# A second buffer for the convolution rows, and two weight loads asked for one pair of heads earlier, in the attention stage of a decoder layer

## The chip, the cores and the metric

The kernel runs on one NeuronCore of a Trainium2 chip. That core has five engines with a queue of instructions each: PE (TensorE, the matmuls), DVE (VectorE), ACT (ScalarE), POOL (GpSimd) and SP (SyncE, which here only issues transfers). Transfers are issued from SP's and POOL's queues and run on the same 16 DMA engines. Every engine works through its queue in order, so an instruction that waits holds up all that stand behind it there. The metric is the device time of the program in microseconds (us), a median over runs.

## The reference

One layer over 1024 tokens of width 1024, in float32. First a mixer: one input projection feeds a sparse attention (8 heads of 64) and, beside it, a short gated convolution over 512 channels; both results are normalised and go through one output projection `w_out`. Then a cross-attention into 256 memory tokens, then a gated feed-forward network of width 2816.

```python
o_nsa  = nsa_attention(q, kc, vc, ks, vs, kw, vw, gates, ...)   # (S, 512)
u      = cc * cx
y      = sum(conv_w[k] * u_pad[:, 2 - k : 2 - k + S] for k in range(3))
o_conv = cb * y                                                 # (S, 512)
merged = concat([rmsnorm(o_nsa), rmsnorm(o_conv)], axis=-1)     # (S, 1024)
h      = merged @ w_out
x      = x + rmsnorm(h)            # then cross-attention, then SwiGLU
```

`w_out` has 1024 rows, so `merged @ w_out` is a sum of two halves: the 512 convolution rows, which are ready before the attention begins, and the 512 attention rows, which are not.

## The kernel before

All large products are made of three matmuls (`mm3`, lines 123 to 125): each operand is split into a high and a low part, and high by high, high by low and low by high are added up. The split takes one ACT copy (line 119) and one subtraction on DVE or POOL (line 120).

The program has these stages: input projections and convolution (up to about 311 us), attention (311 to 566 us), the output projection's attention half together with cross-attention (566 to about 800 us), the feed-forward network (the rest). The change is in the attention stage, and its effects reach the next.

The attention stage has 32 tasks: 8 tiles of 128 tokens, and 4 pairs of heads in each. `run_soft` makes a task's scores on PE (lines 650 and 651), adds the bias and takes the maximum on DVE (656 and 667), takes the exponential on ACT (658 and 688), and divides on POOL (695 for the window part `pwin`, 697 for the selected part `psel`). `pv_stage` transposes these on PE (line 720, into `t`), splits them on ACT and DVE (119 and 120, `pth` and `ptl`) and multiplies by the values (line 726, into `o`). The soft part runs two tasks ahead of the values. At the end of a tile POOL adds up the result `on` (line 738) and SP writes it to DRAM (line 741).

Between these, `fill` does the convolution half of `w_out`: 16 fills, two for each tile of 128 tokens. The first of a pair loads the tile's convolution rows `mhl` (a POOL transfer of 512 KB, line 773). Each fill is 12 matmuls into one bank `f`, an ACT copy to `stg` (line 782), and an SP transfer of `stg` to `pc_d` (line 783). There is one buffer for `mhl`, one for `f` and one for `stg`. `FILL = [5, 7, 10, 10, 12, 13, 13, 16, 16]` says how many fills are written down before each tile's tasks; the last three are written down after task 27.

The weights stand in six buffers named `big`. Four hold `wos[4]` to `wos[7]`, the convolution half, for the whole stage. `load_wo` (line 199) loads `wos[0]` to `wos[3]`, the attention half, 1024 KB each, from POOL's queue. The first two go to the free buffers; `wos[2]` and `wos[3]` take those of `wos[4]` and `wos[5]`, so these two transfers wait until the last fill has read them.

The order of instructions on each engine is not the order of the text. A scheduler places them by a simulated timeline and by the order of the text as priority; `issue_after` keeps a transfer behind a given instruction.

After the attention, `u_load` (lines 869 to 874) brings back, for one tile at a time, the attention result `on`, the fills' sums `pt` (written by `pc_d`) and the residual `x`, all from SP's queue, in the order tile 1, tile 0. `u_merge` splits `on` to `mh` and `ml`, and `u_proj` does 24 matmuls of three in `p` with `wos[0]` to `wos[3]`. These tiles lie in memory that the attention stage has used, so their loads wait for its last readers.

Of the kernel before, what the change touches and what calls it, by code (L numbers as in the profile page):

```python
# [10 lines left out]
F32R = mybir.dt.float32r  # L11
# [6 lines left out]
P = 128  # L18
# [48 lines left out]
def hymba_kernel(ctx: ExitStack, tc: tile.TileContext, a, out: bass.AP):  # L67
# [3 lines left out]
    def pool(st, name, bufs=1, side="left", space=None):  # L71
        kw = {"space": space} if space is not None else {"side": side}
        if space is not DRAM:
            kw["reuse_waits"] = "tile"
        return st.enter_context(tc.tile_pool(name=name, bufs=bufs, **kw))
# [46 lines left out]
    def mm3(ps, lh, ll, rh, rl, start, stop):  # L122
        T.matmul(ps, lh, rh, start=start, stop=False)  # L123
        T.matmul(ps, lh, rl, start=False, stop=False)  # L124
        T.matmul(ps, ll, rh, start=False, stop=stop)  # L125
# [66 lines left out]
    def big_tile():  # L192
        return big.tile([P, 4, 512], F32, name="big")
# [3 lines left out]
    def load_wo(k):  # L197
        wos[k] = big_tile().bitcast(F32R)
        Gp.dma_start(wos[k].rearrange("p a b -> p (a b)"), wo_d[k].rearrange("p x c -> p (x c)"))
# [369 lines left out]
    def group_stat(pl, pn, i, on):  # L569

        sq = pl.tile([P, 4, P], F32, name="sq", bufs=1)
        A.activation(sq, on, AF.Square)
        for c in range(4):
            T.matmul(pn, sq[:, c, :], ones[:, 0:1], start=c == 0, stop=c == 3)
        V.tensor_copy(gn[:, i:i + 1], rsqrt(small, pn, 512, 1, "gn"))


    ap2 = pool(at_stack, "ap2", bufs=2)
    with ExitStack() as st:
# [170 lines left out]
        def run_soft(n):  # L750
            if n >= len(tasks):
                return
            i, h0 = tasks[n]
            g = h0 // 4
            qi, pc, mb = cmps[i]
            if h0 % 4 == 0:
                nts[i, g] = near_stage(i, g, mb)
            yield from soft_stage(n, i, h0, qi, mb, nts[i, g])
            nx = ORD.index(i) + 1
            if h0 == CH and nx < NT:  # L760
                yield
                cmps[ORD[nx]] = cmp_stage(ORD[nx])
# [3 lines left out]
        def fill(m):  # L766

            if m >= 2 * NT:
                return
            i, n = divmod(m, 2)  # L770
            if n == 0:
                mhl = ap2.tile([P, 2, 4, P], F32R, name="mhl", bufs=1)
                Gp.dma_start(mhl.rearrange("p x c t -> p (x c) t"),
                             oc_d[:, :, :, i * P:(i + 1) * P].rearrange("p x c t -> p (x c) t"))
                oct_[i] = (mhl[:, 0], mhl[:, 1])
            mh, ml = oct_[i]
            ps = psf.tile([P, 512], F32, name="f")
            for k in range(4):
                w = wos[4 + k]
                mm3(ps, mh[:, k, :], ml[:, k, :], w[:, n, :], w[:, 2 + n, :], k == 0, k == 3)  # L780
            stg = ap2.tile([P, 512], F32, name="stg", bufs=1)
            A.activation(stg, ps, AF.Copy, scale=rc[:, i:i + 1])
            Y.dma_start(pc_d[i][:, n * 512:(n + 1) * 512], stg)
# [4 lines left out]
        for m in range(FILL[0]):  # L788
            fill(m)
        for n, (i, h0) in enumerate(tasks):  # L790
            ahead = run_soft(n + SKEW)
            pv = pv_stage(i, h0, cmps[i][1], *soft.pop(n))
            steps = next(pv)
            acc = OFF[i]
            for _ in pv:
                acc += RATE[i] / steps
                while acc >= 1:
                    acc -= 1
                    next(ahead, None)
            for _ in ahead:  # L800
                pass
            if n in (9, 21, 29, 30):
                with tc.issue_after(last["norm"].ins):
                    load_wo((9, 21, 29, 30).index(n))
            if h0 == H - 2:
                if i != ORD[-1]:
                    group_stat(ap2, psf.tile([P, 1], F32, name="f"), i, ons[i])
                for m in range(FILL[n // 4], FILL[n // 4 + 1]):
                    fill(m)
        for m in range(FILL[NT], 2 * NT):  # L810
            fill(m)
# [620 lines left out]
```

## Time and profile before

| what | value |
|---|---|
| median of 3 runs | 1412.88 us (1407.75 to 1414.35) |
| profiled execution, device time | 1411.98 us |
| its span in the trace | 1410.2 us |
| PE busy | 1344.6 us, 95% of the span |
| DVE busy | 939.1 us, 67% |
| ACT busy | 683.1 us, 48% |
| POOL busy | 468.1 us, 33% |
| HBM traffic | 143 GB/s over the span |

The span is the time in the trace from the first instruction to the last; some 1.8 us of the device time lie around it. A share of the whole span is a mean over stages that differ, so a stage has to be looked at by itself: which engine is full there, and what PE waits for at its ends. The page also gives the clock that PE was granted, as a share of full speed; its two levels are 2.4 and 1.2 GHz.

### The profile page before, as it was taken

Reading aid. Unit: us, or ns where it says so; the run is one execution under the profiler, and the core shown is the slowest. Engines: PE = TensorE matmul, PEld = TensorE weight load, DVE = VectorE, ACT = ScalarE, POOL = GpSimd, SP = SyncE. Lnnn points to the kernel's source line nnn. Section 1 sums busy time; section 2 is a strip of 40 time slices with the busy share of each in tenths; the row PEclk is TensorE's granted clock in tenths of the full one; section 3 lists DMA queues with packets and bytes.
Section 4 is the critical chain, followed back from the end, with each engine's and each line's share of the span. In section 5 each row is a group of like instructions: output and inputs, shape, how many; then the busy total and the mean of one; then the engine's idle time right before and its main releaser. Section 6 shows DMA issues by size and latency. Waiting matters only on the chain.

```text
span 1410.2 us, 19760 instructions
## 1 busy us (share of the span) xinstructions
PE 1344.6 (95%) x6748; PEld 1125.7 (80%) x6748; DVE 939.1 (67%) x2089; ACT 683.1 (48%) x1465; POOL 468.1 (33%) x454
## 2 busy tenths in 40 slices
PE   8999999999999999798789899999999999989997
PEld 6988888888889888687668688888888887867885
DVE  6544553346889996478886976545454444998787
ACT  5433334337878886356675533332333333444463
POOL 1232332227767664211220076555444531000000
PEclk9999999999999999899899999999999999999999
DMA  7488566495643302953236644432222226930213
GB/s 232 139 281 282 152 219 180 145 256 106 135 83 68 76 9 72 404 190 117 92 98 209 192 152 142 149 124 65 82 83 90 68 90 238 359 112 30 68 60 120
DMA packets 161061, 203.28 MB, mean 144 GB/s; under 512 B 8530, under 2 KB 115198, under 8 KB 156703
## 3 DMA queue, kind: packets, MB, share of 16 engines
q1 hardware_dynamic: 128416, 146.44, 32.3%
q0 software_dynamic: 31392, 53.48, 13.8%
q10 hardware_dynamic: 1152, 2.10, 0.4%
q8 instruction: 53, 0.87, 0.3%
q14 instruction: 48, 0.39, 0.1%
HBM read 138.54 MB, written 63.44 MB: 143 GB/s over the span
## 4 chain that ended last, share of the span: by engine, by line
PE 76%; DVE 13%; ACT 3%; issue 3%; DMA 2%; POOL 1%; SPq 0%; DVEq 0%; POOLq 0%; ACTq 0%
PE m L125 13%; PE m L124 13%; PE m L123 13%; PE mm L123 5%; PE mm L125 5%; PE mm L124 4%; PE o L726 3%; PE t L720 2%; DVE ptl L120 1%; PE s L650 1%; DVE psel L667 1%; PE s L651 1%; PE mm L228 1%; PE tr L485 1%; PE o L124 1%
## 5 line engine op out<-in xcount | busy, mean ns | idle before, releaser
L119 ACT ACTIVATE ah<-raw 128x512 fp32r<-128x512 f32 x132 | 83.0, 631 | 205.7 <-PE m L124 189.7
L125 PE MATMUL mm<-hh,wl 128*128 128x512 f32 x320 | 125.0, 392 | 1.3 <-POOL wl L120 1.3
L123 PE MATMUL mm<-hh,wh 128*128 128x512 f32 x320 | 126.2, 394 | 0.0
L124 PE MATMUL mm<-hl,wh 128*128 128x512 f32 x320 | 125.4, 392 | 0.0
L1169 POOL TENSOR_TENSOR sg<-sg,tmp 128x512 f32<-128x512 f32 x44 | 65.5, 1492 | 177.7 <-ACT sg L1163 67.4
L120 DVE TENSOR_TENSOR al<-raw,ah 128x512 fp32r<-128x512 f32 x120 | 107.6, 899 | 17.2 <-ACT ah L119 17.1
L124 PE MATMUL m<-bl,ah 128*128 128x512 f32 x264 | 102.7, 395 | 3.7 <-DVE bl L120 3.7
L125 PE MATMUL m<-bh,al 128*128 128x512 f32 x264 | 101.1, 394 | 3.0 <-DVE al L120 3.0
L120 POOL TENSOR_TENSOR wl<-wr,wh 128x1024 fp32r<-128x1024 f32 x22 | 54.0, 2454 | 133.2 <-ACT wh L119 133.1
L124 PE MATMUL m<-big,ah 128*128 128x512 f32 x232 | 91.6, 395 | 0.0
L120 DVE TENSOR_TENSOR ptl<-t,pth 128x512 fp32r<-128x512 f32 (+1 forms) x120 | 77.5, 656 | 15.9 <-ACT pth L119 15.8
L119 ACT ACTIVATE pth<-t 128x512 fp32r<-128x512 f32 (+1 forms) x120 | 66.9, 572 | 16.0 <-PE t L720 15.2
L123 PE MATMUL m<-bh,ah 128*128 128x512 f32 x264 | 72.0, 390 | 1.1 <-ACT bh L119 1.1
L125 PEld LDWEIGHTS mm<-hh,wl 128*128 128x128 f32 x320 | 60.5, 189 | 14.9 <-POOL wl L120 2.2
L123 PEld LDWEIGHTS mm<-hh,wh 128*128 128x128 f32 x320 | 60.6, 189 | 12.5
L124 PEld LDWEIGHTS mm<-hl,wh 128*128 128x128 f32 x320 | 60.7, 190 | 12.4
L124 PEld LDWEIGHTS m<-bl,ah 128*128 128x128 f32 x264 | 50.1, 190 | 15.8 <-DVE bl L120 5.3
L125 PEld LDWEIGHTS m<-bh,al 128*128 128x128 f32 x264 | 49.8, 190 | 14.8 <-DVE al L120 4.7
L1168 DVE TENSOR_TENSOR tmp<-m,t 128x512 f32<-128x512 f32 x40 | 27.6, 691 | 50.8 <-PE m L125 22.9
L119 ACT ACTIVATE ah<-q 128x512 fp32r<-128x512 f32 (+2 forms) x55 | 30.0, 545 | 60.5 <-PE m L124 58.6
L123 PEld LDWEIGHTS m<-bh,ah 128*128 128x128 f32 x264 | 49.5, 188 | 12.0 <-ACT bh L119 1.6
L1161 DVE TENSOR_TENSOR sg<-m,t 128x512 f32<-128x512 f32 x40 | 27.6, 691 | 44.4 <-PE m L125 39.6
(497 smaller groups left out, 4130.3 us busy)
## 6 DMA issues: line engine op xcount, KB each, us to landing
raw<-in_ffn_wg_dram SPq DMA_DIRECT2D x52, 256.0 KB, 3.0
raw<-in_ffn_wu_dram SPq DMA_DIRECT2D x52, 256.0 KB, 3.0
hid_d<-sg SPq DMA_DIRECT2D x22, 512.0 KB, 3.1
q<-in_ffn_wd_dram SPq DMA_DIRECT2D x44, 256.0 KB, 5.6
q<-hid_d SPq DMA_DIRECT2D x44, 256.0 KB, 5.4
wr<-in_w_in_dram SPq DMA_DIRECT2D x20, 512.0 KB, 4.5
x<-in_x_dram SPq DMA_DIRECT2D x16, 512.0 KB, 4.5
wo_d<-phl POOLq DMA_DIRECT2D x8, 1024.0 KB, 6.6
```

Of the source, the lines that this page charges most:

```text
L119: A.activation(hi, src, AF.Copy)
L120: (lo_eng or V).tensor_tensor(lo, src, f(hi), OP.subtract)
L123: T.matmul(ps, lh, rh, start=start, stop=False)
L124: T.matmul(ps, lh, rl, start=False, stop=False)
L125: T.matmul(ps, ll, rh, start=False, stop=stop)
L228: T.matmul(ps, rbB[:, h, :], oh, start=True, stop=True)
L485: T.matmul(ph, w1[:, c, :], xv[:, :, n0:n0 + 65, s0], start=c == 0, stop=c == 15)
L720: T.transpose(ps[:, m, j, :], pt[:, j, off * P:(off + 1) * P], ident)
L726: T.matmul(pof, vst[:, kt, b, g, :], t[:, m].rearrange("p h q -> p (h q)"), start=u + x + m == 0, stop=x == 1 and u + m == len(units) - 1)
L1161: V.tensor_tensor(dst, src0, src1, OP.add)
L1168: V.tensor_tensor(tmp, src0, src1, OP.add)
L1169: Gp.tensor_tensor(dst, dst, tmp, OP.mult)
```

## The change

`mhl` gets two buffers, so that the convolution rows of the next tile can be loaded while the fills of the last one still read theirs. And `load_wo` is asked for `wos[2]` after task 28 and `wos[3]` after task 29, where it was after 29 and 30.

```diff
             if n == 0:
-                mhl = ap2.tile([P, 2, 4, P], F32R, name="mhl", bufs=1)
+                mhl = ap2.tile([P, 2, 4, P], F32R, name="mhl", bufs=2)
                 Gp.dma_start(mhl.rearrange("p x c t -> p (x c) t"),
...
-            if n in (9, 21, 29, 30):
+            if n in (9, 21, 28, 29):
                 with tc.issue_after(last["norm"].ins):
-                    load_wo((9, 21, 29, 30).index(n))
+                    load_wo((9, 21, 28, 29).index(n))
```

Neither adds or takes away an instruction. Both move instructions, since the scheduler goes by when a buffer is free. Three places follow, each with the rows of one engine's queue before and then after.

PE, first tile of the attention. `s` are scores against the keys `ks` or `kw`, `t` transposes, `o` products with the values, `f` a fill (`f_2622` is the third, the first that needs the second tile's rows `mhl_2620`). Before:

```order
L650 MATMUL s_2738<-kw_1728,qi_2442 128x128
L651 MATMUL s_2738<-kw_1728,qi_2442 128x128
L708 MATMUL t_2780<-ident_64,pcx_2479 128x128 x2
L726 MATMUL o_2672<-ptl_2715,vst_103 128x256 x2
L650 MATMUL s_2743<-ks_1727,qi_2442 128x128
L651 MATMUL s_2743<-ks_1727,qi_2442 128x128
L650 MATMUL s_2748<-ks_1727,qi_2442 128x128
L651 MATMUL s_2748<-ks_1727,qi_2442 128x128
L123 MATMUL f_2622<-big_2348,mhl_2620 128x512
L124 MATMUL f_2622<-big_2348,mhl_2620 128x512
```

After:

```order
L650 MATMUL s_2687<-kw_1728,qi_2442 128x128
L651 MATMUL s_2687<-kw_1728,qi_2442 128x128
L720 MATMUL t_2709<-ident_64,pwin_2484 128x128 x2
L720 MATMUL t_2709<-ident_64,psel_2483 128x128 x2
L708 MATMUL t_2724<-ident_64,pcx_2479 128x128 x2
L123 MATMUL f_2622<-big_2348,mhl_2620 128x512
L124 MATMUL f_2622<-big_2348,mhl_2620 128x512
```

The third fill now stands 19 rows further up, ahead of five pairs of score matmuls and the first products with the values. On POOL, the load of `mhl_2620` has moved from behind the divisions of the first two tasks to directly behind the load of the first tile's rows.

PE, the end of the attention: the beginning of the last fill, `f_5765`. `psel_5816` belongs to the last but one task, `pwin_5939` and `psel_5938` to the last. Before:

```order
L720 MATMUL t_6122<-ident_64,pwin_5939 128x128 x3
L726 MATMUL o_6034<-ptl_6110,vst_103 128x256
L720 MATMUL t_6122<-ident_64,pwin_5939 128x128
L720 MATMUL t_6136<-ident_64,pwin_5939 128x128 x2
L720 MATMUL t_6136<-ident_64,psel_5938 128x128 x2
L123 MATMUL f_5765<-big_2348,mhl_5747 128x512
L124 MATMUL f_5765<-big_2348,mhl_5747 128x512
```

After:

```order
L720 MATMUL t_6056<-ident_64,pwin_5817 128x128
L726 MATMUL o_5781<-ptl_6024,vst_103 128x256
L720 MATMUL t_6056<-ident_64,pwin_5817 128x128
L720 MATMUL t_6056<-ident_64,psel_5816 128x128 x2
L720 MATMUL t_6069<-ident_64,psel_5816 128x128 x4
L123 MATMUL f_5765<-big_2348,mhl_5747 128x512
L124 MATMUL f_5765<-big_2348,mhl_5747 128x512
```

The last fill has moved up by one task. From its end to the first matmul of `p` there were 14 transposes and 23 products; now there are 34 and 46.

POOL, the same stretch; `wo_d2_84` and `wo_d3_85` are the sources of `wos[2]` and `wos[3]`, and `on_5905` is the last tile's result. Before:

```order
L697 TENSOR_SCALAR psel_5938<-psel_5938,sm_5941 128x1024 x2
L773 DMA mhl_5747<-oc_d_77 128x8x128
L738 TENSOR_TENSOR on_5905<-otmp_6027 64x256 x2
L199 DMA big_6032<-wo_d2_84 128x2048
L199 DMA big_6115<-wo_d3_85 128x2048
L738 TENSOR_TENSOR on_5905<-otmp_6197 64x256 x2
L816 DMA big_6203<-wq_d0_78 128x2048
```

After:

```order
L697 TENSOR_SCALAR psel_5940<-psel_5940,sm_5943 128x1024 x2
L738 TENSOR_TENSOR on_5905<-otmp_6029 64x256
L199 DMA big_5906<-wo_d2_84 128x2048
L738 TENSOR_TENSOR on_5905<-otmp_6029 64x256
L199 DMA big_6034<-wo_d3_85 128x2048
L738 TENSOR_TENSOR on_5905<-otmp_6197 64x256 x2
L816 DMA big_6203<-wq_d0_78 128x2048
```

The load of the last tile's convolution rows is gone from here (it stands 47 rows further up, among the divisions of the fifth tile). The two weight loads still stand behind the last division, one now between the two halves of an `on`. The order on SP from the last `pc_d` to the loads of `on`, `pt` and `x` for the next stage is the same in both.

## Rows read from the trace of the kernel before

**Rows 1.** The page: span, and busy time by engine.

```profile
span 1410.2 us, 19760 instructions
PE 1344.6 (95%) x6748; PEld 1125.7 (80%) x6748; DVE 939.1 (67%) x2089; ACT 683.1 (48%) x1465; POOL 468.1 (33%) x454
```

**Rows 2.** Windows: stretch, length, engines' busy time, granted clock, DMA share, GB/s.

```profile
311.00:350.00 39.00, 36.06 (x234) 32.35 (x233) 26.67 (x149) 27.67 (x88) 23.65 (x39) 0.96 0.57 108
...
450.00:500.00 50.00, 47.92 (x355) 45.04 (x354) 48.98 (x186) 41.37 (x96) 33.30 (x40) 1.00 0.31 69
500.00:550.00 50.00, 48.26 (x345) 43.90 (x344) 44.51 (x154) 42.99 (x95) 31.14 (x35) 1.00 0.05 17
...
650.00:700.00 50.00, 38.52 (x231) 33.16 (x230) 43.80 (x110) 35.51 (x107) 9.34 (x11) 0.90 0.27 96
700.00:750.00 50.00, 43.02 (x224) 35.83 (x224) 37.68 (x74) 32.63 (x81) 10.94 (x10) 0.90 0.42 135
```

**Rows 3.** Chain that ended last, pieces: start, length, what.

```profile
324.96 5.17 DMA mhl<-oc_d
...
564.57 6.08 DMA on<-on_d
```

**Rows 4.** Timeline of PE, 328 to 331 us: start, length, idle before in brackets.

```profile
328.50 0.28 PE L651 MATMUL s<-ks,qi 128*128 128x128 f32 x1
330.18 0.50 PE L123 MATMUL f<-big,mhl 128*128 128x512 f32 x1 [1.40 <-DMA mhl<-oc_d]
```

**Rows 5.** Timeline of POOL: two loads of `mhl`, and of `wos[2]`, `wos[3]`.

```profile
324.96 0.95 POOL L773 DMA_DIRECT2D mhl<-oc_d  x1
...
548.43 0.96 POOL L773 DMA_DIRECT2D mhl<-oc_d  x1
...
559.23 1.25 POOL L199 DMA_DIRECT2D big<-wo_d  x2 [7.69 <-PE f L125]
```

**Rows 6.** Timeline of PE, 560 to 578 us.

```profile
560.63 0.40 PE L125 MATMUL f<-big,mhl 128*128 128x512 f32 x1
...
565.29 0.28 PE L726 MATMUL o<-ptl,vst 128*128 128x256 f32 x1
571.35 0.80 PE L123 MATMUL p<-big,mh 128*128 128x512 f32 x1 [5.78 <-ACT mh L119]
...
573.22 0.63 PE L123 MATMUL p<-big,mh 128*128 128x512 f32 x1
573.64 0.63 PE L124 MATMUL p<-big,mh 128*128 128x512 f32 x1
...
577.02 0.40 PE L123 MATMUL p<-big,mh 128*128 128x512 f32 x1
577.25 0.39 PE L124 MATMUL p<-big,mh 128*128 128x512 f32 x1
```

**Rows 7.** Timeline of SP's queue, 545 to 565 us.

```profile
545.71 16.44 SPq L783 DMA_DIRECT2D pc_d<-stg  x3
562.25 0.46 SPq L870 DMA_DIRECT2D on<-on_d  x1
564.19 0.32 SPq L872 DMA_DIRECT2D pt<-pc_d  x1
```

**Rows 8.** DMA, 558 to 575 us: GB/s in 40 slices, the two queues.

```profile
GB/s 386 29 0 0 0 58 251 0 308 386 386 463 366 424 405 328 308 386 443 443 284 357 405 453 439 381 400 429 419 424 443 395 424 342 178 439 390 386 439 390
...
q0 software_dynamic: 386, 2.90, 50.0%
q1 hardware_dynamic: 1048, 2.70, 42.1%
```

**Rows 9.** Transfers of `on`, then of `pc_d`: issue to landing.

```profile
DMA to landing us min/median/max: 2.0/8.7/10.1
...
DMA to landing us min/median/max: 2.0/5.0/6.2
```

**Rows 10.** Waits, 311 to 575 us: total, times, longest.

```profile
ACT stg L782 <- DMA pc_d<-stg: 2.8, 2, 1.9
```

## The prediction, made before the result was known

> **What bounds the kernel now.** I read the page first: PE is busy for 95% of the span [rows 1], so time can come back only where PE stands still or runs at the lower clock, and only if nothing else is full there. The windows by stage come next [rows 2]. The reader is to see two things in them. From 450 to 500 us DVE is busy for 48.98 of 50 us, more than PE with 47.92: both are full, and a transfer that comes sooner gives nothing there. At the stage's two ends DVE has room (26.67 of 39 us from 311 to 350), and DMA is nearly unused before the last end (0.05 of the engines, 17 GB/s, from 500 to 550).
>
> Then the chain that ended last. In the attention stage two transfers stand on it: one of `mhl` at 324.96 us and one of `on` at 564.57 us [rows 3]. They are the two places that this change can reach, and PE's timeline shows what they cost. At 330.18 us the third fill begins after 1.40 us without work, waiting for `mhl` [rows 4]. At the end the last product with the values begins at 565.29 us and takes 0.28 us; the first matmul of `p` begins at 571.35 us, after 5.78 us of idle time [rows 6]. The matmuls behind it run at the lower clock level, 1.2 GHz: 573.22 to 573.64 us is 0.42 us from one to the next, 577.02 to 577.25 us is 0.23 us [rows 6].
>
> Last, why `on` was late. SP issues the fills' last `pc_d` just before 562.25 us, then the first `on`, then `pt` at 564.19 us; the second `on` goes out at 564.57 us [rows 3, 7]. POOL issues both weight loads at 559.23 us, having waited 7.69 us for the last fill [rows 5]. From about 561 us on the DMA engines move some 390 GB/s without a pause [rows 8]. The two weight loads are 2.1 MB; what SP had asked for up to the second `on` (`pc_d` 0.26, `on` 0.26, `pt` 0.52, `on` 0.26) is 1.3 MB. So `on` travels in a queue, not alone: 6.08 us, where the fastest `on` took 2.0 us [rows 3, 9].
>
> **The change, part by part.** No instruction is added or removed, so busy time stays; the sum is of waits. It is made against the profiled execution, 1412.0 us (a span of 1410.2 us and 1.8 us around it), which lies 0.9 us under the median of the runs, 1412.9 us.
>
> First fills. With two buffers the second tile's rows are asked for at about 305 us instead of 324.96 us, so the wait of 1.40 us goes [rows 4, 5]: -1.4 us. What is late next is `stg`, which still has one buffer: a fill's copy waits for the transfer of the fill before, 5.0 us in the median [rows 9], and the fills now follow each other sooner. Before, this was two waits of 2.8 us together, on ACT [rows 10], whose exponentials and splits queue behind the copy. I count the third to the fifth fill and the last two as likely to wait 0.5 to 1 us more each, of which PE feels a third, since transposes already in its queue go on: +1.2 us, between 0 (ACT's waits are covered) and +4 us (all of them reach PE).
>
> The middle. Fills keep their place to within some 30 matmuls. Where PE and DVE are both full [rows 2] I take 0. The bounds are -2 us (all that PE stands still from 450 to 500 us) and +2.8 us (one fill, 12 matmuls of 0.23 us, set ahead of scores for which DVE waits).
>
> Last fills. The last load of `mhl` went out at 548.43 us, behind the last divisions [rows 5]; now it stands 47 rows earlier, and the last fill can run one task earlier. Behind the last fill there are now 80 matmuls of the value part where there were 37. Those 37 took 4.7 us (560.87 to 565.57 us [rows 6]), so the 80 take some 10 us. `wos[4]` and `wos[5]` are therefore free about 11 us before the end of the attention, not 6, and the two weight loads go out then, when DMA is nearly idle, and need 5.4 us (2.1 MB at 390 GB/s), which ends before `pt` and the second `on` are asked for. Asking at tasks 28 and 29 alone would only let POOL wait longer; it is the earlier fill that makes the request worth something. The loads stand behind the last division, so nothing that PE needs is queued behind their wait.
>
> The boundary. `pt` still waits for the last transposes, 1.4 us before the attention's end, and `on` follows it. With the weights out of the way, 0.79 MB at 390 GB/s take 2.0 us, and with the 2.0 us of a transfer that is alone [rows 9] `on` lands at 564.19 + 4.0 = 568.2 us where it landed at 570.65 us: -2.4 us. Bounds: 0 (`on` is held by something that the chain doesn't name) and -4.1 us (2.0 us instead of 6.08).
>
> The Trainium skill ("DMA: Bandwidth & Descriptors", section "Queues, rings and completion order") says that each DMA engine takes turns between the queues that have work for it, packet by packet. By that rule SP's 1.3 MB would have had half the rate: 6.7 us from 561.8 us and 2 us of latency give 570.5 us, and the row has 570.65 us; both queues moved nearly the same (2.90 and 2.70 MB [rows 8]). The trace agrees, and by the same rule the landing without the weights is the 568.2 us above.
>
> The clock. Thirteen matmuls of `p` ran at the lower level, 0.42 instead of 0.23 us each: 2.6 us [rows 6]. With 3.4 us of idle time instead of 5.8 I take a third of it back, -0.9 us, between 0 and -2.6.
>
> Sum: -1.4 + 1.2 + 0 - 2.4 - 0.9 = -3.5 us, or 1409.4 us against the median. The next stage then starts 3.5 us earlier, with its order changed in some two dozen small places; I take 0 for it, and its bounds are in the rivals.
>
> **The rivals.** *The wait is taken up elsewhere.* `on` still stands behind `pt` and the first `on`; if the rest of the DMA work (5.60 MB in 17 us [rows 8]) fills the gap that the weights leave, and `stg` takes the start's gain, the result is -0.5 us: 1412.4 us. For it speaks that the engines are full to the end of that stretch; against it, that `wq` and all that follows on POOL is asked for only after the last `on` is added up, later than the loads on the chain.
>
> *Slower: fills ahead of scores.* The scheduler now puts the third to fifth fill before scores that DVE waits for. Each is 2.8 us on PE; DVE starts its later tasks up to 8.3 us later, and from 450 to 500 us it has hardly any room to catch up [rows 2]. If all of it stays, less the 1.4 us and the 3.3 us of the boundary, +3.6 us are left (8.3 - 1.4 - 3.3). PE would then wait for scores and fall to the lower clock as it did after 565 us; one and a half times that loss, 3.9 us, makes +7.5 us: 1420.4 us. The change is slower as soon as more than 4.7 us of the delay survive until POOL is past the last divisions, at 548 us [rows 5]. Against it: PE loses nothing while it does fills, and in 311 to 350 us DVE stood still for 12 of 39 us anyway.
>
> *Faster: the next stage.* From 650 to 750 us the granted clock is 0.90 [rows 2]: a fifth of 100 us at half speed, 10 us lost, and PE is busy for only 81.5 of the 100 us. There short waits decide on the clock, and another order and start can spare some of them. Two thirds of that loss on top of the forecast: 1402.7 us. Nothing in the trace says that the new order is better rather than worse, so this is a spread to both sides.
>
> *The change does nothing there*, because `mhl` still comes late, can be left out: for the last tile its transfer stands 47 rows of POOL further up than before.
>
> **How the numbers follow.** Chances: the forecast 0.43, taken up elsewhere 0.23, slower 0.13, faster by the next stage 0.21. What a measurement of this kernel can tell from no change is about 0.5%, 7 us, as far apart as its three runs lie. Faster than that (under 1405.8 us) is most of the last case, and a little of the forecast: 0.20. Slower (over 1420 us): 0.10, some of the slow case ending under it. Within: 0.70. The range reaches down past the faster case and up to where half of the slower one is in: 1401 to 1418 us. The forecast's own range is 1404 to 1415 us: its bounds add up to -10 and +7 us, and not all of them will fall to one side.
>
> **What would show it.** Right: no wait of `f` for `mhl` at 330 us; the weight loads on POOL some 11 us before the last product with the values; DMA busy between 550 and 560 us; the second `on` landing in about 4 us, and PE's wait for `mh` 3 to 3.5 us. Wrong: `on` still taking 6 us or more; more than 6 us of ACT waiting on `pc_d`; DVE standing still for longer than before between 450 and 500 us; or a difference that lies behind 600 us, which none of my terms is about.

## The result: the changed kernel is slower

The changed kernel takes 1427.1 us (1423.9 to 1430.2 in six runs), the kernel before 1412.3 us (1407.8 to 1414.4 in six): a ratio of 1.011, interval 1.0095 to 1.0125. The forecast was 1409.4 us, its range 1401 to 1418. The page of the profiled execution after answers to [rows 1]; the engines are as busy in sum, but for PE's 6 us more.

```profile
span 1425.6 us, 19754 instructions
PE 1350.5 (95%) x6748; PEld 1128.9 (79%) x6748; DVE 937.9 (66%) x2089; ACT 683.5 (48%) x1465; POOL 468.4 (33%) x454
```

**Where the 15 us are.** PE does the same matmuls in both kernels, so the traces can be laid on each other by work done: each matmul has the price of its form at full speed (0.23 us for 512 columns, 0.12 for 256, 0.09 for a transpose), the prices are added up in each kernel's own order, and the lag is how much later a kernel has done the same amount. Other prices move it by up to 0.5 us. One execution differs from the next by more: `e2` (below), whose instructions stand as in the kernel before, lies up to 0.7 us off it, and `e4`, the same up to the last fills, up to 1.1 us. The profiles differ by up to 3 us at 311 us already, ahead of all that is edited; that is taken off. Times at the top are those of the kernel before.

```
lag of PE, us, at            338   356   398   490   540   584   680   830
changed kernel              -1.5   3.8   3.5   8.2   7.7   3.5  10.7  14.8
```

So there are five pieces: a gain of 1.5 us at the first fills; 5.3 us lost by 356 us; 4.2 us lost between 398 and 540; 4.2 us gained at the boundary; and 11.3 us lost in the next stage, behind everything that the edit names.

**The gain at the start came.** The third fill begins without a wait; in [rows 4] it had 1.40 us.

```profile
326.43 0.48 PE L123 MATMUL f<-big,mhl 128*128 128x512 f32 x1
```

**The first loss.** The chain of waits of the changed kernel shows POOL's issue of one load and the transfer of another near 335 us; in [rows 3] its transfer was one of `mhl`, at 324.96 us (start, length, what):

```profile
335.24 0.95 POOL mhl L773
...
336.19 8.20 DMA qi<-q_d
...
344.53 0.27 PE s L592
```

`qi` are the queries of the next tile (line 588), here the third. They have two buffers, so the load waits until the last scores of the first tile are made. POOL's timeline, first two rows of the kernel before (the load of the second tile's rows is in [rows 5]), then the changed one:

```profile
329.08 1.14 POOL L588 DMA_DIRECT2D qi<-q_d  x1 [3.17 <-PE s L651]
330.58 1.04 POOL L606 TENSOR_TENSOR pc<-pc,csm 128x512 f32<-128x512 f32 x1 [0.36 <-DVE sm L692]
```

```profile
310.69 0.88 POOL L773 DMA_DIRECT2D mhl<-oc_d  x1 [5.37 <-PE mm L125]
...
325.20 0.95 POOL L773 DMA_DIRECT2D mhl<-oc_d  x1
329.74 1.04 POOL L606 TENSOR_TENSOR pc<-pc,csm 128x512 f32<-128x512 f32 x1 [3.59 <-DVE csm L605]
...
334.00 1.28 POOL L120 TENSOR_TENSOR pcx<-pc,pcx 128x512 fp32r<-128x512 f32 x1
335.24 0.95 POOL L773 DMA_DIRECT2D mhl<-oc_d  x1
336.19 1.14 POOL L588 DMA_DIRECT2D qi<-q_d  x1
```

The queries are asked for 7.1 us later. PE's timeline of the changed kernel shows when the scores that they wait for are made, and what the lateness costs:

```profile
334.50 0.28 PE L651 MATMUL s<-ks,qi 128*128 128x128 f32 x1
...
342.61 0.39 PE L726 MATMUL o<-pth,vst 128*128 128x256 f32 x1 [0.61 <-ACT pth L119]
...
344.53 0.27 PE L592 MATMUL s<-kcst,qi 128*128 128x64 f32 x1 [1.30 <-DMA qi<-q_d]
...
346.22 0.40 PE L592 MATMUL s<-kcst,qi 128*128 128x64 f32 x1
346.44 0.40 PE L593 MATMUL s<-kcst,qi 128*128 128x64 f32 x1
```

The last scores of the first tile begin at 334.50 us, behind the third and fourth fill; before, at 328.50 [rows 4]: 6.0 us later. On POOL the load has moved back as well. It stood ahead of the product for `pc` (line 606) and waited 3.17 us for the scores; now it stands behind that, behind a task's divisions and behind `pcx`, on which POOL is busy to 335.28 us, half a microsecond longer than the last scores take (to 334.78). So POOL's own work ends last, by little, and the late scores alone would hold the load nearly as long; no run holds the one and frees the other. The last 0.95 us are the load of the fourth tile's rows, which now stands just ahead of the queries on POOL. From 345.5 us on the matmuls go at half the pace (0.21 us apart, then 0.11 again from 352): PE fell to the lower clock level behind these waits.

**The second loss.** DVE's waits from 380 to 500 us (total, times, longest), of the kernel before and of the changed one:

```profile
DVE psel L667 <- PE s L651: 1.5, 4, 0.5
DVE pwin L656 <- PE s L651: 1.1, 1, 1.1
```

```profile
DVE pc L599 <- PE s L593: 3.7, 3, 2.4
DVE psel L667 <- PE s L651: 3.6, 4, 2.1
...
DVE pwin L656 <- PE s L651: 1.5, 2, 1.1
```

DVE waits 8.8 us for scores where it waited 2.6. In PE's order fills 9, 10, 11 and 12 stand ahead of 2, 4, 6 and 6 pairs of score matmuls against `ks` and `kw` that they stood behind, and fills 9 and 10 ahead of 8 and 2.5 pairs against the compressed keys (lines 592 and 593) too. DVE's longest wait is for those, behind fill 10:

```profile
398.87 0.23 DVE L599 CUSTOM_DVE_ANT_0 pc<-s,ct 128x64 f32<-128x64 f32 x1 [2.42 <-PE s L593]
```

The windows that answer to [rows 2] have DVE 3.0 us short from 311 to 350 us, 1.9 us from 450 to 500, and busier from 500 to 550; PE's clock in the next stage is down to 0.79:

```profile
311.00:350.00 39.00, 35.54 (x210) 31.72 (x210) 23.67 (x134) 23.57 (x74) 21.04 (x36) 0.90 0.70 117
450.00:500.00 50.00, 46.92 (x340) 42.83 (x339) 47.05 (x173) 39.87 (x94) 32.19 (x38) 1.00 0.47 90
500.00:550.00 50.00, 48.66 (x350) 44.38 (x349) 47.13 (x175) 44.35 (x97) 31.69 (x37) 1.00 0.03 12
650.00:700.00 50.00, 38.22 (x222) 32.35 (x222) 39.37 (x97) 34.42 (x101) 8.52 (x11) 0.90 0.23 85
700.00:750.00 50.00, 36.78 (x189) 30.40 (x188) 41.09 (x87) 33.25 (x89) 11.82 (x10) 0.79 0.31 95
```

**The boundary came as forecast, 7 us late.** POOL's weight loads, SP's transfers, and PE (answering to [rows 5 to 7]):

```profile
561.22 0.61 POOL L199 DMA_DIRECT2D big<-wo_d  x1
...
562.59 0.57 POOL L199 DMA_DIRECT2D big<-wo_d  x1
```

```profile
571.23 0.32 SPq L872 DMA_DIRECT2D pt<-pc_d  x1
571.60 0.42 SPq L870 DMA_DIRECT2D on<-on_d  x1
```

```profile
572.57 0.28 PE L726 MATMUL o<-ptl,vst 128*128 128x256 f32 x1
576.04 0.49 PE L123 MATMUL p<-big,mh 128*128 128x512 f32 x1 [3.20 <-ACT mh L119]
...
577.90 0.63 PE L123 MATMUL p<-big,mh 128*128 128x512 f32 x1
578.33 0.63 PE L124 MATMUL p<-big,mh 128*128 128x512 f32 x1
...
581.64 0.40 PE L123 MATMUL p<-big,mh 128*128 128x512 f32 x1
581.88 0.39 PE L124 MATMUL p<-big,mh 128*128 128x512 f32 x1
```

The last product is 7.28 us later than in [rows 6], the first matmul of `p` only 4.69. PE waits 3.20 us instead of 5.78, and some eight matmuls run at the lower level (0.43 us apart) instead of thirteen: 2.6 of the 4.2 us are the wait, the rest is the clock.

### The profile page after: what moved, and what is told of

Its sections match the earlier page's. It is cut to its first block, busy times and chain, and to the rows that moved or that the text cites. A ratio compares the mean times of both kernels' runs of the same rounds, so it can differ in the third digit from the quotient of the medians.

```text
span 1425.6 us, 19754 instructions
## 1 busy us (share of the span) xinstructions
PE 1350.5 (95%) x6748; PEld 1128.9 (79%) x6748; DVE 937.9 (66%) x2089; ACT 683.5 (48%) x1465; POOL 468.4 (33%) x454
## 4 chain that ended last, share of the span: by engine, by line
PE 78%; DVE 12%; issue 3%; ACT 3%; DMA 2%; POOL 1%; SPq 0%; DVEq 0%; POOLq 0%; ACTq 0%
PE m L125 13%; PE m L124 13%; PE m L123 13%; PE mm L123 6%; PE mm L125 6%; PE mm L124 6%; PE o L726 2%; PE t L720 2%; DMA x<-in_x_dram 1%; DVE ptl L120 1%; PE s L650 1%; PE s L651 1%; DVE psel L667 1%; PE mm L228 1%; PE tr L485 1%
```

## The experiments

Each kernel was timed beside the kernel before. The interval of its ratio to it stands with each, and the lags of their profiles (to be read as above) in one table at the end of this section. "Order held" means that the instructions of a stage are chained, engine by engine, in a given order, by dependences that carry no semaphore; in such kernels every instruction has line 76, that of the helper that records it.

```diff
+        for x, y in zip(at, at[1:]):
+            tc.add_manual_dep(logs[k][y], logs[k][x].name,
+                              mybir.DependencyInfo(mybir.DependencyClass.NoSync, mybir.DependencyReason.DATA),
+                              reason="order")
```

Here `logs[k]` lists the instructions of one engine as they are written down, and `at` is the order to hold.

**The two edits apart.** First theory: the second buffer alone costs it. `e1` has only the buffers, `e2` only the requests.

```diff
-            if n in (9, 21, 28, 29):
+            if n in (9, 21, 29, 30):
```

> Two buffers for the convolution rows, the weight blocks asked for as before (tasks 29 and 30). Theory: the whole loss comes from the second buffer, which lets the third to fifth fill stand ahead of scores; only one row of POOL's queue differs from the changed kernel, so attention ends at 572.5 us (573 within 1 us) and the time is the changed kernel's, 1427 us (1423 to 1431). Rival, the earlier requests cost it (weight blocks in the way of on and x): 1412 us or less.

> One buffer, the weight blocks asked for after tasks 28 and 29. Theory: the requests still stand behind the last division and wait for the last fill, no row of any queue moves against the kernel before, so 1412 us (1408 to 1416) and weight loads at 559 us. Rival, the earlier requests cost the 15 us: 1420 us or more.

Measured: 1426.4 us (1.0098 to 1.0132) and 1410.4 us (0.9993 to 1.0012). The buffers are the whole effect. The earlier requests move no instruction of any engine: they wait for the last fill in either case.

**The last fills alone.** `e4` has the early load only where the forecast needed it.

```diff
-                mhl = ap2.tile([P, 2, 4, P], F32R, name="mhl", bufs=2)
+                mhl = ap2.tile([P, 2, 4, P], F32R, name="mhl" if i < 7 else "mhe", bufs=1)
```

> One buffer for the rows of the first seven tiles, one of its own for the last tile's; requests after tasks 28 and 29. Only the last fills move. Theory, that the loss of the attention comes from the first fills: the attention ends at 565.5 us within 0.5, the boundary gives its 3 us (on lands in about 4 us, PE waits 3 us for mh). The next stage tells two things apart: if its 11 us in the changed kernel come from being late, 1409 us; if they come from its changed order (80 rows of PE and of DVE moved) it loses here too, 1413 to 1420 us.

Measured: 1409.8 us (0.9983 to 1.0007). The attention is level, and the boundary gives 3 us that last. (The lag of -5.8 us at 584 passes: the lower clock level, which the kernel before has from 570 to 577 us, comes here only at 592 us.) The next stage, in an order that is neither the old nor the changed kernel's, takes as long as before: 268.8 us for the work of the windows below. That speaks for lateness or for the changed kernel's own order, and the next four kernels take the next stage apart.

**The next stage: order or lateness?** `p1` is the changed kernel with the next stage's order held as before; `p4` the inverse.

> The changed kernel, with the instructions behind the attention stage (those written after line 818) held on every engine in the order that they have in the kernel before; the attention stage is the changed one. In the changed kernel PE is 3.7 us behind at 580 us and 15 us behind at 830 us. If the 11 us come from the changed order of the next stage: attention ends at 572 to 573 us as in the changed kernel, then PE stays about 4 us behind, 1415 to 1418 us. Rival, that they come from being late (transfers of x and on that meet others, the clock): 1424 us or more.

> The inverse: the kernel before, with the instructions behind the attention stage held in the order of the changed kernel. If the order costs the 11 us: attention ends at 565.5 us, time 1419 to 1423 us. Rival, that lateness costs it: 1409 to 1413 us.

Measured: 1415.7 us (1.0018 to 1.0041) and 1422.0 us (1.0061 to 1.0091). Both fall where the order was to put them: of the 15 us, 11 are the order of the next stage, wherever the attention ends. Windows from the first matmul of `p` to the same piece of work in the feed-forward network, of the kernel before, of `p4` and of the changed kernel:

```profile
571.40:840.00 268.60, 239.34 (x1197) 198.30 (x1198) 205.25 (x408) 151.37 (x374) 56.32 (x49) 0.93 0.53 178
```

```profile
569.20:848.80 279.60, 245.81 (x1197) 203.60 (x1198) 203.29 (x408) 151.77 (x374) 57.45 (x49) 0.90 0.51 171
576.00:855.00 279.00, 242.62 (x1197) 200.62 (x1198) 205.26 (x408) 151.87 (x374) 60.61 (x55) 0.91 0.51 172
```

The same 1197 matmuls take 11.0 us more in `p4`: 4.5 us of standing still (33.8 against 29.3 us) and 6.5 us of longer matmuls (245.8 against 239.3 us busy, mean clock 0.90 against 0.93). In the changed kernel the shares are the other way round, 7.1 and 3.3 us. The sum is steady: this work takes 267 to 269 us in all eleven kernels whose next stage has the order of before, and 279 to 280 in the three with the changed order (the changed kernel, `e1`, `p4`). The waits of PE that grew most in the windows of the kernel before and of `p4` are those of the transposes for `pr`, the normalised probabilities of the cross-attention:

```profile
PE s L972 <- DVE pr L958: 3.6, 3, 3.0
```

```profile
PE s L76 <- DVE pr L76: 6.8, 4, 4.0
```

Which engine's order carries it? `r4` changes PE's alone, `r6` DVE's and ACT's alone.

> The kernel before, with PE's order behind the attention stage as in the changed kernel, and the other engines as before. If PE's own order carries the 11 us of the next stage: 1418 us or more. If it is the order on DVE and ACT: 1410 to 1414 us.

> The inverse: DVE and ACT behind the attention stage in the order of the changed kernel, PE, POOL and SP as before. If DVE's and ACT's order carries the 11 us: 1418 us or more. If it is PE's: 1410 to 1414 us. If both kernels of this pair are slow, it is the two orders not fitting each other, and neither engine alone.

Measured: 1423.1 us (1.0077 to 1.0107) and 1425.2 us (1.0086 to 1.0119). Both are as slow as the whole changed order or slower, so the two kernels do not say which engine carries it: an order that is changed on one side alone no longer fits the other side's, and that may cost as much by itself. The whole changed order, in which all engines come from one schedule, costs the same, and what makes it slow stays open. The lag grows in several steps of 1 to 5 us between 600 and 810 us, not at one place.

**The attention: the order or the buffer?** `p5` has both edits, with PE, DVE and ACT held in the order of before through the program; `q4` the same, but with the last fills where the early load lets them stand (the order of `e4`), and the next stage held.

> Two buffers and the earlier requests, but PE, DVE and ACT keep the order of the kernel before through the whole program (POOL and SP are left to the scheduler, and differ in the one load of the last tile's rows). If the second buffer costs only by the order that it brings: 1409 to 1412 us, attention's end at 564 to 566 us, no wait longer than before. Rival, that the second buffer itself costs (its place in memory, its transfers beside the queries'): 1417 us or more.

> Two buffers and the earlier requests, with PE, DVE and ACT held in the order of the kernel that moved only the last fills, and the next stage in the order of the kernel before. If order is all that the change cost, both gains are left: the third fill's wait (1.4 us) and the boundary (3 us): 1405 to 1408 us. Rival, that the first gain is taken up by the wait for divisions or by the copies of stg: 1408 to 1410 us.

Measured: 1411.5 us (0.9994 to 1.0014) and 1407.8 us (0.9974 to 0.9997). The buffer costs nothing where it moves nothing. `q4` keeps the boundary's gain; the first fill's 1.7 us are there at 338 us and gone at 346 us. What takes them is neither of the two that its rival named, but mostly the clock: PE waits once, 0.47 us up to 336.69 us, and the granted clock is at the lower level from 338.2 to 341.6 us, which costs half of these 3.4 us.

```profile
338.00:342.00 4.00, 4.00 (x20) 3.82 (x19) 3.53 (x25) 2.75 (x9) 1.79 (x4) 0.57 0.16 30
```

**The early stall.** `e3` keeps the second tile's load behind the second task's division; `q1` lets it go early but holds the third fill's first matmul behind the first tile's last scores (next stage held).

```diff
-                Gp.dma_start(mhl.rearrange("p x c t -> p (x c) t"),
...
+                with tc.issue_after(last["norm"].ins) if i == 1 else ExitStack():
+                    Gp.dma_start(mhl.rearrange("p x c t -> p (x c) t"),
...
```

```diff
+    tc.add_manual_dep(logs["T"][hold["fill"]], hold["score"].name,
+                      mybir.DependencyInfo(mybir.DependencyClass.NoSync, mybir.DependencyReason.DATA), reason="hold")
```

> The changed kernel, but the load of the second tile's rows is kept behind the division of the second task, where it stood before. Theory: the stall behind the load of the queries (4.8 us from 338 to 355 us) goes: queries asked for at about 329 us, no wait of the scores for them; the later fills still stand ahead of scores, so 2 to 3 us stay; attention ends at 567 to 569 us, and the time is 1419 to 1424 us if the next stage keeps its 11 us. Rival, that only the lateness of DVE from 400 to 500 us counts and the early stall is absorbed: attention still ends at 571 to 573 us, 1427 us.

> The changed kernel with the next stage in the order of the kernel before, and the first matmul of the third fill kept behind the last scores of the first tile, where it stood before (its rows are loaded early, as in the changed kernel). The later fills stay where the change put them. Theory: in the changed kernel the queries of the third tile were asked for 7.1 us later because the last scores of the first tile, which free their buffer, stood behind the third and fourth fill. Held, they go out at 329 to 331 us, PE is 1 to 2 us ahead of the kernel before at 340 us and not 4 us behind at 360 us; what the later fills cost (3.5 to 4 us between 400 and 500 us) stays, the boundary gives 3.3 us: 1408 to 1411 us. Rival, that the queries were late for POOL's own order or for the shared transfers: still 4 us behind at 360 us, 1414 to 1417 us.

Measured: 1423.6 us (1.0071 to 1.0118) and 1412.9 us (0.9997 to 1.0027). `e3` said little: the queries went out at 330.6 us and their stall was gone, but the held load now stood beside the third tile's, and the third fill waited 2.0 us for its rows. `q1` is cleaner: queries at 329.6 us, 1.0 us behind at 356 us instead of 4.2 in `p1`, and 2.7 us less in all by the medians, less than expected (the two intervals overlap a little). The scheduler put the load of the queries back ahead of `pc` on POOL there, so `q1` moves the scores and POOL's order at once.

Then a miss that helped. `q3` gives the second tile's rows a buffer of their own and nothing else (next stage held); it was to show the early stall alone, and it changed much of the attention's order besides.

```diff
+                mhl = ap2.tile([P, 2, 4, P], F32R, name="mhe" if i == 1 else "mhl", bufs=1)
```

> A buffer of its own for the second tile's rows only; next stage in the order of the kernel before; the last load of the rows and the weight blocks as in the kernel before. Theory: the early stall (4 to 5 us behind at 360 us) and nothing given back at the boundary: 1414 to 1417 us. If the early lateness also brings the loss from 400 to 500 us: 7 us behind at the end of the attention, 1417 to 1420 us.

Measured: 1407.3 us (0.9966 to 0.9990), faster than the kernel before. That gain is mostly from the middle, not from the start: it is level at 356 us, and between 398 and 540 us, where the changed kernel loses 4.2 us, it gains 2.8, with fills 7 to 13 within four pairs of score matmuls of their old places. Fills 3 to 5 stand as early as in the changed kernel and the queries go out late too (335.49 us), yet PE waits only a moment, and the clock stays:

```profile
342.63 1.05 PE L76 MATMUL s<-kcst,qi 128*128 128x64 f32 x8 [0.39 <-DMA qi<-q_d]
```

So late scores were not the whole cause of the early stall. In `q3` no load of rows stands just ahead of the queries. `r1` tests that by itself: the changed kernel's order on every engine in the attention, but for this one pair on POOL; to be compared with `p1`.

> The changed kernel's order on every engine in the attention stage, but for one pair on POOL: the load of the third tile's queries stands ahead of the load of the fourth tile's rows (in the changed kernel behind it); next stage in the order of the kernel before. To be compared with the same kernel without the swap, 1415.7 us. Theory: the two loads share the transfer engines and the rows go first, so the queries land 1 to 2 us later than they need; with the swap PE's wait of 1.3 to 1.9 us shrinks to under 0.5, PE stays at the higher clock level behind 345 us, and 2 to 4 us come back: 1412 to 1414 us. Rival, that only the scores behind the fills make the queries late: 1415 to 1416 us.

Measured: 1411.6 us (0.9994 to 1.0016), 4.0 us under `p1` (3.4 by the two ratios). POOL's and PE's timelines of `r1`:

```profile
334.93 1.22 POOL L76 DMA_DIRECT2D qi<-q_d  x1
336.15 0.87 POOL L76 DMA_DIRECT2D mhl<-oc_d  x1
```

```profile
342.31 0.39 PE L76 MATMUL o<-pth,vst 128*128 128x256 f32 x1 [0.61 <-ACT pth L76]
...
342.78 1.87 PE L76 MATMUL s<-kcst,qi 128*128 128x64 f32 x16
```

The queries go out one issue (0.95 us) sooner after the work ahead of them on POOL, and land in 7.1 us instead of the changed kernel's 8.2: PE does not wait for them. The windows of 338 to 346 and 346 to 354 us, first of the changed kernel (whose attention `p1` shares), then of `r1`, show what the wait had cost:

```profile
338.00:346.00 8.00, 6.08 (x43) 5.49 (x42) 4.38 (x21) 5.59 (x20) 4.07 (x9) 0.97 1.29 204
346.00:354.00 8.00, 8.00 (x45) 8.00 (x46) 5.36 (x30) 5.22 (x14) 3.30 (x6) 0.61 0.09 34
```

```profile
338.00:346.00 8.00, 7.39 (x60) 7.02 (x59) 5.85 (x39) 5.86 (x21) 4.78 (x11) 1.00 1.33 194
346.00:354.00 8.00, 7.82 (x61) 7.39 (x60) 7.53 (x30) 7.96 (x25) 4.71 (x6) 1.00 0.14 44
```

PE stands still for 1.9 of 8 us in the changed kernel and for 0.6 in `r1`; the eight us behind have a granted clock of 0.61, here 1.00. One pair of loads in the wrong order is 1.3 us of waiting and some 3 us of clock.

**The later fills.** `q2` has two buffers from the fourth tile on only (next stage held).

```diff
+                mhl = ap2.tile([P, 2, 4, P], F32R, name="mhe" if i in (3, 5, 7) else "mhl", bufs=1)
```

> Two buffers only from the fourth tile on (tiles 4, 6 and 8 use one of their own); next stage in the order of the kernel before. The first six fills stand where they stood, the later ones where the change put them or close to it. Theory, that the later fills, set 2 to 6 scores ahead, cost by themselves: level with the kernel before at 400 us, 3 to 4 us behind at 500 us, the boundary gives 3 us back: 1409 to 1412 us. Rival, that the loss from 400 to 500 us is the early lateness passed on: no loss at 500 us, 1407 us or less.

Measured: 1413.7 us (1.0014 to 1.0040), 2 us more than expected. The profile has it 1.4 us ahead at 398 us and 4.2 us behind at 490 us, though nothing was late before: the later fills cost this by themselves, and it is not the early lateness passed on. Its lag ends at 0.1 us, where the timed runs are 3.2 us apart. The rest lies outside the table: 0.9 us ahead of 311 us, 0.7 us behind 1200 us, and the profiled execution of the kernel before is 1.6 us slower than the median of the runs beside `q2`.

**Towards a better kernel.** `p3` is `e4` with the next stage held; `r2` gives the second and the last tile a buffer of their own, next stage held.

> The kernel with a buffer of its own for the last tile's rows (only the last fills move), with the instructions behind the attention stage in the order of the kernel before. If the order of the next stage took back 3 us of the 5 us that this kernel had gained at 591 us: 1406 to 1408 us, 3.5 to 5 us under the kernel before. Rival, that the gain at the boundary is lost there in any order because DVE and DMA are full: 1409 to 1411 us.

> A buffer of its own for the rows of the second and of the last tile, next stage in the order of the kernel before. If the gains of the two kernels that gave one each add up (1407.3 and 1407.9 us, both some 3 us under the kernel before): 1404 to 1406 us. Rival, that the scheduler's new order in between takes one of them back: 1407 to 1411 us.

Measured: 1407.9 us (0.9978 to 0.9999) and 1408.4 us (0.9974 to 0.9994). `p3` fell where the order theory put it, but its profile ends where that of `e4` does (-2.8 and -3.0 us) and the two intervals overlap, so it does not show that the order of `e4` had cost anything. In `r2` the two gains do not add up: the fills between moved again, and it was 3.9 us behind at 356 us. `q3`, `q4`, `p3` and `r2` are all faster than the kernel before, by 2 to 3 us, with intervals that end at 0.9999 or under; they can't be told apart.

```
lag of PE, us, at            338   356   398   490   540   584   680   830
p1 changed, next held       -1.7   4.2   3.9   8.1   7.5   3.3   4.9   3.2
r1 p1, one pair swapped     -0.5   0.6   0.2   5.2   4.6   0.4   2.2   0.1
q1 p1, third fill held      -1.2   1.0   0.5   4.9   4.3   0.9   0.9   0.9
q2 from fourth tile         -0.4  -0.4  -1.4   4.2   3.6   0.1   2.1   0.1
q3 second tile only         -1.5   0.0  -0.8  -3.8  -3.6  -5.2  -3.4  -5.3
q4 order held               -1.7   0.4   0.5   1.2   1.2  -3.2  -0.6  -2.7
p3 last tile, next held     -0.1  -0.1  -0.1   0.2   0.2  -3.0  -0.7  -2.8
e1 buffers alone            -1.5   4.2   3.8   8.4   7.8   4.6  11.1  15.2
e2 requests alone            0.6   0.7   0.7  -0.1  -0.1  -0.5  -0.6  -0.6
e4 last tile                 1.1   1.1   0.9   0.3   0.3  -5.8  -0.9  -3.0
e3 second load held          2.3   3.4   2.8   8.1   7.5   4.0   7.7  12.1
p4 before, next changed      0.1   0.1   0.2   0.5   0.5   0.5   6.3  11.4
p5 all orders as before     -0.2   0.4   0.2  -0.5  -0.5  -0.4  -0.4  -0.3
r2 second and last tile     -1.3   3.9   3.6   0.2   0.4  -2.8  -2.8  -2.7
r4 next changed on PE        0.5   0.5   0.3   0.9   0.9   0.7  10.7  11.5
r6 next changed on DVE, ACT  0.3   0.3   0.1   0.5   0.5   0.6   9.6  14.6
```

## Why the prediction was wrong

**First fills: right, but for what comes next.** The wait of 1.40 us went, though the rows were asked for at 310.69 us and not at 305: POOL waited 5.37 us for the projections. "What is late next is `stg`" was wrong: the +1.2 us for it did not come. In the changed kernel ACT never waits for `pc_d`, and the copy's waits are for the fill itself:

```profile
ACT stg L782 <- PE f L125: 12.0, 9, 3.0
```

What was late next was the load of the queries. The prediction compared where `mhl` stood on POOL, and looked for what its transfers would fill, but not which load the fourth tile's rows had passed, nor what the score matmuls behind the fills set free: the queries' buffer. `r1` gives the pair alone 3.4 to 4.0 us; no term or bound had it.

**The middle: the failed bound.** It was taken as 0, at most +2.8 us for one fill ahead of scores. Four fills moved that way and some 4 to 5 us were lost (`q1`, `q2`, `r1` from 398 to 540 us), with DVE waiting 6 us longer for scores. The bound on the other side fails too: `q3` and `r2`, with other places for the same fills, gain 2.8 and 3.2 us there.

**Last fills, boundary and clock: right.** Forecast: weight loads 11 us ahead of the last product, measured 11.4 and 10.0. The second `on` was to land 4.0 us after SP asks for `pt`; it had landed 4.1 us after (571.23 to 575.36 us) by ACT's timeline:

```profile
575.36 0.63 ACT L119 ACTIVATE mh<-on 128x512 fp32r<-128x512 f32 x1 [0.70 <-DMA on<-on_d]
```

By the rule of turns between queues in the Trainium skill ("DMA: Bandwidth & Descriptors", section "Queues, rings and completion order") it would be the same 4.0 us once the weights are out of the way; the trace agrees, but with one queue at work (POOL's moved 0.01 of 1.42 MB from 570 to 576 us) it can't tell this rule from another. PE's wait was 3.2 us (3 to 3.5). The two terms were -3.3 us; the lag falls by 4.2 from 540 to 584 us here and by 3.2 to 4.4 in `p3` and `q4`. The wait gave 2.6 us (-2.4 forecast), the clock some 1.6 (-0.9 forecast). Only "DMA busy between 550 and 560 us" fell, as all was 7 us late. The request at tasks 28 and 29 gained nothing by itself, as the prediction said.

**The next stage: the step that decided.** "With its order changed in some two dozen small places; I take 0 for it." Some 80 of PE's matmuls and 90 of DVE's operations are set elsewhere in their order, and they cost 11 us (`p1`, `p4`), where the term was nothing. The prediction named the risk, "a spread to both sides", and then priced only its fast side, as a rival of -6.7 us with 0.21; the slow side had no case. Four other orders of the same work cost 8 (`e3`), 11 (`r4`, `p4`) and 14 us (`r6`) over the windows above, one costs nothing (`e4`), and none was better. So nought was the best case here, not the middle one; which places make an order slow is open. Of the four signs of being wrong that the prediction named, two came: DVE standing still for longer from 450 to 500 us, and a difference behind 600 us.

**The slower rival** had the right beginning, fills ahead of scores, and a fitting size for the attention (4 to 5 us of its 8.3 stay). But it went by DVE alone and knew neither the queries nor the 11 us behind; 1420.4 us was too little, and a chance of 0.13 too low.

**The range.** The bound of +7 us leaves out the start's own -1.4 us; with it the upper bounds add up to +5.4. The measured +15 us lies beyond either.

Without the next stage the account closes: -1.5 at the start, +5.3 with the stall, +4.2 for the later fills (-0.3 between them), -4.2 at the boundary make +3.5 us; `p1` was measured 2.5 to 5.8 us over the kernel before.

## What to carry to other kernels

Where a scheduler places instructions by when a buffer is free, a second buffer is first of all a new order: compare every queue as a whole, ask of each load that moved up which load it has passed, and of each matmul what buffer it sets free. Take a changed order behind the edit as a cost with a slow side, not as zero: of five other orders here, four were 8 to 14 us slower and one was level. To see what an edit is worth by itself, hold the order of the rest: here that turned a kernel 15 us slower into one 2 to 3 us faster (`q4`).

## What was not expected of the hardware

PE stood still for 0.61 us and then 1.30 us in the changed kernel, and the granted clock was at the lower level from 345.5 to 352.3 us; with 0.61 us alone (`r1`) it stayed at the higher one. The wait itself was the smaller half of the loss. The same came three more times: in `p1`, `e1` and `r2` a wait of 0.6 us and one of 1.9, 1.7 and 1.2 us were followed by 6.8 us at the lower level, in `r2` behind a wait that was not for the queries. But the length of the waits alone doesn't decide: in `q4` a single wait of 0.47 us was followed by 3.4 us at the lower level, and these runs do not show what does. In the next stage too part of the 11 us, 3.3 (changed kernel) to 6.5 us (`p4`), is longer matmuls, though no wait behind its first matmul is longer than 4.1 us.
